# A hybrid decoder block on one core: a pinned first tile with zero products, first keys in double banks, and token sums whose low parts move to VectorE

## The chip, the core and the metric

The kernel runs on one core of a Trainium2 chip. The metric is the device time of one execution in microseconds; the time before is 1198.09, the median of three runs (1197.95 to 1198.48). PE is the matrix engine (TensorE), DVE is VectorE, ACT is ScalarE, POOL is GpSimd, SP is SyncE, which here only issues DMAs. A tile's name stands for its buffer; L95 is line 95 of the kernel before.

## What is computed

One layer: 16 meta tokens are put ahead of 512 tokens of width 1024, then

```
hn  = rmsnorm(h, norm_mix_pre)
rq, rk, rv, rg, sq, sk, sv, ga, gb = split(hn @ w_in)
y_ret = (silu(rg) * groupnorm(retention(rotary(rq), rotary(rk), rv))) @ w_ret_out
y_sb  = stick_breaking(sq, sk, sv) @ w_sb_out
h = h + rmsnorm((sigmoid(ga) * y_ret + sigmoid(gb) * y_sb) @ w_out, norm_mix_post)
h = h + rmsnorm(swiglu(rmsnorm(h, norm_ffn_pre)), norm_ffn_post)
```

with 4 retention heads (keys 256, values 512), 16 attention heads of 64 and an inner width of 2816. All is float32.

## The kernel before, in words

**Products in two parts.** Every operand is kept as a high part (the float32 number rounded to PE's fast form) and a low part (what is left). ACT makes the high part by a copy, DVE the low part by a subtraction (`split` at L103, `lo_of` at L100). One product is three on PE: high by high, high by low, low by high (L126 and L134, all issued at L95). Weights come in raw tiles of up to 1 MB (pool `wraw`, two buffers) and are split into units `wh` and `wl` (pool `wun`, five buffers of each). A raw buffer is free when all that reads it is done, a unit when PE has used it last; the next load or split waits for that.

**The order.** The program is written once and a scheduler with a timing model sets each engine's order, in which the engine then works strictly in sequence. Instructions marked with `tc.keep_in_program_order` stay in the order of the code. In the attention part all of PE is pinned so.

**The start (L648 to L715).** Gains of the first norm are brought into all partitions by transposes (`grow`, `gcol`, `gps`, L678 to L685). `innorm(i)` (L660) takes 128 tokens: ACT squares and sums a row (L666), DVE and POOL make the reciprocal root (L147, L148), DVE scales (hx, L671), PE transposes, and `split` writes the columns into hT and hL. Then come the values: `Values.load` loads 256 columns of w_in for four heads (L433), `part` multiplies one tile of tokens (L439), and `tail` the meta tokens. The first pair's queries and keys follow (`qk_work`, L487): queries in one PSUM bank of 512, keys in two halves of 264, evacuated by ACT into qa, qb, ka, kb and by DVE into the low parts, among them kl. Banks come from `bank_p` (two of 512) and from `bank_a` (two double ones).

**Token sums (L153 to L191).** The retention projections use a seven-product scheme on quarters, for which sums t1 to t4 of the normalised tokens are needed, split into th and tl. For each of four rows of feature tiles, `row_steps` issues ten POOL steps of 128x256 (L175) on hT and hL, then one ACT copy of 128x1024 (th, L184) and four POOL subtractions (tl, L185 and L186). These steps are handed out eight at a time between the attention's output products (L798 to L804), whose results DVE multiplies by a gate (gb, L801). The next user, `rv_proj(0)`, calls `tok_quarters` (L219): its four POOL sums in place, L233 to L236, prepare the weights' sums in the raw tiles. Its first two products use tokens as they are (`PRODUCTS`, L193), the third needs weights s2 and tokens t2. Then `ret_qk` (L898) multiplies and rotates queries and keys (`rotate`, L879: products with cosT and sinT into tiles rt, which read a PSUM bank that PE wants back), and the gate's `tok_quarters` makes its sums on POOL (L244, tile st).

**The tail (L1242 to L1257).** For each tile of 128 tokens the last products of two halves run; ACT squares and sums each half (L1249), DVE multiplies it by the last gains (fo, L1250), then the two sums make rs (L1252, L1253 on POOL), DVE finishes both halves (L1256) and SP writes them out.

Of the kernel before, what the change touches and what calls it, by code (L numbers as in the profile page):

```python
# [10 lines left out]
F32 = mybir.dt.float32  # L11
F32R = mybir.dt.float32r
# [4 lines left out]
P = 128  # L17
# [17 lines left out]
def hybrid_block(  # L35
# [32 lines left out]
    def bank_p():  # L68
        turns_p[0] += 1
        pool = third[0] if third and turns_p[0] % 3 == 0 else ps_p  # L70
        return pool.tile([P, 512], F32, tag="p", name="pp")

    def bank_a():
        return ps_a.tile([P, 2, 512], F32, tag="a", name="pa")
# [23 lines left out]
        return keep(nc.tensor.transpose(dst, src, idn))  # L98

    def lo_of(lo, src, hi):  # L100
        nc.vector.tensor_tensor(lo, src, hi.bitcast(F32), op=ALU.subtract)  # L101

    def split(hi, lo, src):  # L103
        ins = nc.scalar.activation(hi, src, AF.Copy)  # L104
# [48 lines left out]
    class Tokens:  # L153
# [15 lines left out]
        def row_steps(self, k, t, u):  # L169

            b11, b12, b21, b22 = [[v[:, k, :].bitcast(F32) for v in self.quarter(i, j)] for i in range(2) for j in range(2)]
            t1, t2, t3, t4 = [t[:, n, :] for n in range(4)]

            def op(d, p, q, o):
                tc.keep_in_program_order(nc.gpsimd.tensor_tensor(d, p, q, op=o))  # L175
# [8 lines left out]
            nc.scalar.activation(self.th[:, :, k, :], t, AF.Copy)  # L184
# [212 lines left out]
    with tc.tile_pool(name="s2", bufs=2, side=RS, reuse_waits="tile") as s2:  # L397
# [29 lines left out]
        class Values:  # L427
# [5 lines left out]
            def load(self):  # L433
# [2 lines left out]
                self.vt = vts[c] = s2.tile([P, NT, 4, P], F32R, tag="vt", name="vt")  # L436
                self.units = load_units(src, KD, 256, [(0, 4, 0, 256), (4, 4, 0, 256)])

            def part(self, js):  # L439
# [44 lines left out]
        qks = {}  # L484
        flat = lambda t: t.rearrange("p a b -> p (a b)")

        def qk_work(work, p, what="qk"):  # L487
            def q_load():
                return feat_units(w_in[:, O_SQ + P * p : O_SQ + P * (p + 1)])

            def q_steps(us):
                ps = bank_p()
# [12 lines left out]
            def k_steps(us):  # L505
                ka = s2.tile([P, 2, 264], F32R, tag="ka", name="ka", bufs=1)
                kb = s2.tile([P, 2, 264], F32R, tag="kb", name="kb")
                kl1 = kl1s[p % 2]
                for i in range(2):
                    cs = slice(264 * i, 264 * (i + 1))  # L510
                    pk = bank_p()[:, :264]
# [4 lines left out]
                    nc.scalar.activation(kb[0:64, i], pk[64:128], AF.Copy)  # L516
# [137 lines left out]
        def xload(i):  # L654
            if i == NT:
                nc.sync.dma_start(xts[i][:NM], meta)
            else:
                nc.sync.dma_start(xts[i], x[i * P : (i + 1) * P, :])

        def innorm(i):  # L660
            n = NM if i == NT else P
            c0 = 0 if i == NT else NM + i * P
            xt = xts[i]
            junk = bank_a().rearrange("p a b -> p (a b)")
            ss = cst.tile([P, 1], F32, name=f"ss{i}")
            nc.scalar.activation(junk[:n], xt[:n], AF.Square, accum_out=ss[:n])  # L666
            rstd_of(ss[:n], ss[:n], 1e-6, 1.0 / D, n)
            for j in range(2):
                hx = s2.tile([P, 512], F32, tag="qb", name="hx")
                cs = slice(512 * j, 512 * (j + 1))  # L670
                nc.vector.scalar_tensor_tensor(hx[:n], xt[:n, cs], ss[:n], gps[:n, j, :], op0=ALU.mult, op1=ALU.mult)  # L671
# [6 lines left out]
        nc.sync.dma_start(grow, g_mix_pre.rearrange("o (k p) -> (o k) p", p=P))  # L678
        xload(0)

        pg = bank_b()
        turned(pg[:, :KD], grow, ident[:KD, :KD])
        nc.scalar.activation(gcol, pg[:, :KD], AF.Copy)
        for k in range(KD):
            turned(gps[:, k // 4, (k % 4) * P : (k % 4 + 1) * P], gcol[:, k : k + 1].to_broadcast([P, P]), ident)  # L685
        vals = [Values(0), Values(1)]
        innorm(0)
        vals[0].load()
        xload(1)
        vals[1].load()  # L690
        innorm(1)
        for i in range(2, NT + 1):
            xload(i)
        work = Work()
        qk_work(work, 0)
        for j in range(NT):
            for v in vals:
                for _ in v.part((j,)):
# [73 lines left out]
    with tc.tile_pool(name="s3", bufs=1, side=RS, reuse_waits="tile") as s3:  # L772
# [20 lines left out]
        for f in range(0, KD, 2):  # L793
            if f:
                us = feat_units(w_sb_out[:, P * f : P * (f + 2)])
            gb = s3.tile([P, 2, T], F32, tag="gb", name="gb", bufs=2)
            nc.sync.dma_start(gb, gb_d[:, f : f + 2, :])
            for e in range(2):  # L798
                ps = bank_p()
                feat_mm(ps, us[e], lambda k: yh[:, k, :], lambda k: yl[:, k, :])  # L800
                nc.vector.tensor_tensor(gb[:, e, :], ps, gb[:, e, :], op=ALU.mult)  # L801
# [401 lines left out]
    with tc.tile_pool(name="s8", bufs=2, side=RS, reuse_waits="tile") as s8:  # L1203
# [38 lines left out]
        for i in range(NT):  # L1242
            sc, fo = [col("sc0"), col("sc1")], s8.tile([P, D], F32, tag="fo", name="fo")
            for c in range(2):
                for f in range(NF - REST, NF):
                    product(i, c, f)
                cs = slice(512 * c, 512 * (c + 1))
                sq = s8.tile([P, 512], F32, tag="sq", name="sq")
                nc.scalar.activation(sq, banks[i][c], AF.Square, scale=D**-0.5, accum_out=sc[c])  # L1249
                nc.vector.tensor_tensor(fo[:, cs], banks[i][c], gfin[:, cs], op=ALU.mult)  # L1250
            rs = col("rs")
            nc.vector.scalar_tensor_tensor(rs, sc[0], 1e-6, sc[1], op0=ALU.add, op1=ALU.add)  # L1252
            nc.gpsimd.tensor_tensor(rs, rs, nhalf, op=ALU.pow)  # L1253
            for c in range(2):
                cs = slice(512 * c, 512 * (c + 1))
                nc.vector.scalar_tensor_tensor(fo[:, cs], fo[:, cs], rs, h2[:, i, cs], op0=ALU.mult, op1=ALU.add)  # L1256
                nc.sync.dma_start(out[i * P : (i + 1) * P, cs], fo[:, cs])  # L1257
# [43 lines left out]
```

## Time and profile before

| | |
|---|---|
| median of three runs | 1198.09 us |
| profiled execution | 1197.83 us, its span 1196.0 us |
| PE busy | 1168.3 us (98%) |
| DVE busy | 851.2 us (71%) |
| ACT busy | 529.8 us (44%) |
| POOL busy | 348.7 us (29%) |
| mean granted clock of PE | 0.997 |

The page gives busy times and the slices of the span; the views by window give the same for single stretches. A timeline row has start, duration, engine, line, operation, tile out<-in, shape and count, and in brackets the engine's idle time ahead of it and what ended it. A row of the waits has the engine that waited and for whom, then us in total, times, and the longest.

### The profile page before, as it was taken

How to read it: one execution, taken by the hardware profiler on the slowest of the kernel's cores; microseconds unless marked ns; L12 is line 12 of the kernel's file. 1: busy time of each engine (PE TensorE's matmuls, PEld its weight loads, DVE VectorE, ACT ScalarE, POOL GpSimd, SP SyncE). 2: the span in 40 equal slices, each digit the busy share in tenths (PEclk: the TensorE clock that was granted, in tenths of full speed). 3: DMA queues.
4: the chain of work that ended last, by engine and by line, in shares of the span. 5: the costliest groups of instructions: out<-in, count | busy, mean ns of one | idle time of the engine just before them, and what ended most of it. 6: DMA issues, size and time to landing. Idle time of an engine off the chain costs nothing.

```text
span 1196.0 us, 18637 instructions
## 1 busy us (share of the span) xinstructions
PE 1168.3 (98%) x7521; PEld 1058.4 (88%) x7521; DVE 851.2 (71%) x1120; ACT 529.8 (44%) x899; POOL 348.7 (29%) x374
## 2 busy tenths in 40 slices
PE   7999999999999999999999999999999999999997
PEld 7988999988888988988898898788999999998886
DVE  5588788887447865687577657776799999983333
ACT  5476676666223434334243424344354444443321
POOL 2011122125864401340341120001366666620000
PEclk9999999999999999999999999999999999999999
DMA  6222222233532224122222414334132333253311
GB/s 196 84 85 89 63 64 73 75 99 110 190 116 71 81 71 141 36 81 100 78 73 79 141 54 141 132 135 139 44 106 81 114 98 130 84 185 106 103 39 71
DMA packets 98055, 118.24 MB, mean 99 GB/s; under 512 B 2584, under 2 KB 74272, under 8 KB 97968
## 3 DMA queue, kind: packets, MB, share of 16 engines
q1 hardware_dynamic: 97536, 115.98, 30.0%
q8 instruction: 59, 0.97, 0.3%
q10 hardware_dynamic: 432, 1.07, 0.3%
q14 instruction: 28, 0.23, 0.1%
HBM read 109.96 MB, written 7.08 MB: 98 GB/s over the span
## 4 chain that ended last, share of the span: by engine, by line
PE 76%; DVE 9%; POOL 6%; issue 4%; ACT 2%; DMA 2%; DVEq 0%; POOLq 0%; SPq 0%; ACTq 0%
PE pp L95 34%; PE pb L95 17%; PE pa L95 15%; PE pc L95 5%; DVE wl L101 3%; PE px L95 3%; PE pb L98 3%; DMA raw<-in_w_in_dram 2%; POOL ts L175 2%; POOL tl L175 2%; ACT wh L104 1%; DVE sm L574 1%; POOL raw L244 1%; POOL st L244 1%; DVE ub L266 1%
## 5 line engine op out<-in xcount | busy, mean ns | idle before, releaser
L101 DVE TENSOR_TENSOR wl<-raw,wh 128x1024 fp32r<-128x1024 f32 x196 | 265.9, 1363 | 79.5 <-ACT wh L104 76.1
L104 ACT ACTIVATE wh<-raw 128x1024 fp32r<-128x1024 f32 x196 | 196.9, 1013 | 209.0 <-PE pa L95 78.0
L95 PE MATMUL pp<-hT,wh 128*128 128x512 f32 (+1 forms) x320 | 116.5, 364 | 1.3 <-DVE qb L101 1.1
L95 PE MATMUL pp<-hL,wh 128*128 128x512 f32 (+1 forms) x320 | 112.3, 351 | 0.0
L95 PE MATMUL pp<-hT,wl 128*128 128x512 f32 (+1 forms) x320 | 112.1, 350 | 0.0
L101 DVE TENSOR_TENSOR wl<-st,wh 128x1024 fp32r<-128x1024 f32 x54 | 84.8, 1575 | 15.6 <-ACT wh L104 15.5
L244 POOL TENSOR_TENSOR st<-raw 128x512 f32<-128x512 f32 x28 | 43.6, 1579 | 159.8 <-DMA raw<-in_w_in_dram 159.8
L95 PE MATMUL pp<-qk,wh 128*128 128x512 f32 x256 | 83.2, 399 | 2.0 <-ACT qk L104 1.7
L95 PE MATMUL pp<-wh,hT 128*128 128x256 f32 (+1 forms) x240 | 75.0, 313 | 0.7 <-ACT hT L104 0.7
L95 PE MATMUL pp<-wh,hL 128*128 128x256 f32 (+1 forms) x240 | 74.4, 310 | 0.8 <-DVE ss L147 0.8
L95 PE MATMUL pp<-wl,hT 128*128 128x256 f32 (+1 forms) x240 | 73.9, 308 | 0.0
L104 ACT ACTIVATE wh<-st 128x1024 fp32r<-128x1024 f32 x54 | 56.0, 1055 | 35.5 <-POOL st L244 17.2
L95 PEld LDWEIGHTS pp<-hT,wl 128*128 128x128 f32 x320 | 60.2, 188 | 8.3
L584 POOL CAST mg<-sp 128x32 fp32r<-128x32 f32 x32 | 7.4, 230 | 204.5 <-DVE sp L575 155.1
L95 PEld LDWEIGHTS pp<-hT,wh 128*128 128x128 f32 x320 | 60.2, 188 | 7.5 <-issue 1.3
L95 PE MATMUL pa<-hT,wh 128*128 128x264 f32 (+1 forms) x192 | 62.4, 325 | 2.8 <-DVE rt L891 2.8
L95 PEld LDWEIGHTS pp<-hL,wh 128*128 128x128 f32 x320 | 60.4, 189 | 5.3
L574 DVE TENSOR_TENSOR_SCAN sm<-sm,mask 128x528 f32<-128x528 f32 (+1 forms) x64 | 54.9, 858 | 12.5 <-ACT sm L571 11.6
L148 POOL TENSOR_TENSOR rs<-rs,nhalf 128x1 f32<-128x1 f32 x20 | 12.7, 636 | 170.7 <-DVE rs L147 170.7
L95 PE MATMUL pa<-hL,wh 128*128 128x264 f32 (+1 forms) x192 | 62.2, 324 | 0.0
L95 PE MATMUL pa<-hT,wl 128*128 128x264 f32 (+1 forms) x192 | 62.1, 324 | 0.0
L95 PEld LDWEIGHTS pp<-qk,wh 128*128 128x128 f32 x256 | 47.6, 188 | 13.4 <-ACT qk L104 2.4
(326 smaller groups left out, 3726.8 us busy)
## 6 DMA issues: line engine op xcount, KB each, us to landing
raw<-in_w_in_dram SPq DMA_DIRECT2D x28, 1024.0 KB, 5.0
raw<-in_w_ffn_in_dram SPq DMA_DIRECT2D x22, 1024.0 KB, 5.1
raw<-in_w_in_dram SPq DMA_DIRECT2D x32, 512.0 KB, 4.2
raw<-in_w_ffn_out_dram SPq DMA_DIRECT2D x11, 1024.0 KB, 4.9
raw<-in_w_ret_out_dram SPq DMA_DIRECT2D x8, 1024.0 KB, 5.0
raw<-in_w_sb_out_dram SPq DMA_DIRECT2D x4, 1024.0 KB, 5.2
raw<-in_w_out_dram SPq DMA_DIRECT2D x4, 1024.0 KB, 5.0
ysb<-in_x_dram SPq DMA_DIRECT2D x4, 512.0 KB, 8.7
```

Of the source, the lines that this page charges most:

```text
L95: return keep(nc.tensor.matmul(*args, **kw))
L98: return keep(nc.tensor.transpose(dst, src, idn))
L101: nc.vector.tensor_tensor(lo, src, hi.bitcast(F32), op=ALU.subtract)
L104: ins = nc.scalar.activation(hi, src, AF.Copy)
L148: nc.gpsimd.tensor_tensor(dst, dst, nhalf[:n], op=ALU.pow)
L175: tc.keep_in_program_order(nc.gpsimd.tensor_tensor(d, p, q, op=o))
L244: nc.gpsimd.tensor_tensor(d[:, k : k + 2], p[:, k : k + 2], q[:, k : k + 2], op=op)
L266: nc.vector.tensor_tensor(ub[:, 1:4:2, :], p.rearrange("p (o n) -> p o n", o=1).to_broadcast([P, 2, n]), ub[:, 1:3, :], op=ALU.add)
L574: nc.vector.tensor_tensor_scan(rev, rev, mask[:, r0:][:, ::-1], 0.0, op0=ALU.mult, op1=ALU.max)
L584: nc.gpsimd.tensor_copy(g[:, two, 0:NM], m)
```

## The change

There are five parts.

1. **The first tile.** The first load of values goes out in two DMAs of 512 KB (`begin`) ahead of the second tile of tokens, and the gains' load moves from SP's queue to ACT's. The first tile's norm is shared: ACT squares half a row, DVE the other half, without the multiply-add step between. Its steps on ACT and DVE are pinned in a written order: square, first half of the weights, the tile, second half of the weights, then the second tile's square.
2. **Zero products.** Five products of zeros (128x512) on PE ahead of the gains' transposes, four behind them, into a bank that nothing reads.
3. **First keys.** Both halves of the first pair's keys go into `bank_a` (double banks); the queries stay in `bank_p`.
4. **Token sums.** The four POOL subtractions of a row become one DVE subtraction of 128x1024. A row has 11 steps handed out, not 14, and six go out at a time.
5. **The tail.** rs is made before the second half is multiplied by the gains.

```
 in row_steps:
             nc.scalar.activation(self.th[:, :, k, :], t, AF.Copy)
-            for n in range(4):
-                yield op(self.tl[:, n, k, :], t[:, n, :], self.th[:, n, k, :].bitcast(F32), ALU.subtract)
+            yield lo_of(self.tl[:, :, k, :], t, self.th[:, :, k, :])
...
-                for _ in range(8):
+                for _ in range(6):
                     next(token_sums, None)
 the start:
+            if i == 0:
+                so = cst.tile([P, 1], F32, name="so")
+                jv = s2.tile([P, 512], F32, tag="qb", name="jv")
+                tc.keep_in_program_order(nc.scalar.activation(junk[:, 0:512], xt[:, 0:512], AF.Square, scale=D**-0.5, accum_out=ss))
+                nc.vector.scalar_tensor_tensor(jv, xt[:, 512:D], 1.0 / D, xt[:, 512:D], op0=ALU.mult, op1=ALU.mult, accum_out=so)
+                nc.vector.scalar_tensor_tensor(ss, ss, 1e-6, so, op0=ALU.add, op1=ALU.add)
+                nc.gpsimd.tensor_tensor(ss, ss, nhalf, op=ALU.pow)
+                return
...
+        def first_tile(v):
+            pin = tc.keep_in_program_order
+            norm(0)
+            los = [v.take(0)]
...
+            los[0]()
+            for j in range(2):
+                ks = slice(4 * j, 4 * j + 4)
+                hi, lo = [v_[:, ks, NM : NM + P] for v_ in (hT, hL)]
+                pin(nc.scalar.activation(hi, pts[j], AF.Copy))
+                pin(lo_of(lo, pts[j], hi))
+            v.take(1)()
+            norm(1)
...
+        def idling(n):
+            for _ in range(n):
+                tc.keep_in_program_order(nc.tensor.matmul(idle, zeros[:, 0:P], zeros, start=True, stop=True))
+        idling(5)
...
+        idling(4)
+        first_tile(vals[0])
...
+        def first_bank():
+            kp.append(None)
+            return bank_a()[:, 0, :] if len(kp) > 1 else bank_p()
+        qk_work(work, 0, first_bank)
 the tail, in the loop over the two halves c:
                 nc.scalar.activation(sq, banks[i][c], AF.Square, scale=D**-0.5, accum_out=sc[c])
+                if c:
+                    rs = col("rs")
+                    nc.vector.scalar_tensor_tensor(rs, sc[0], 1e-6, sc[1], op0=ALU.add, op1=ALU.add)
+                    nc.gpsimd.tensor_tensor(rs, rs, nhalf, op=ALU.pow)
                 nc.vector.tensor_tensor(fo[:, cs], banks[i][c], gfin[:, cs], op=ALU.mult)
```

Here `v.take(i)` issues the high part of half i of the weights on ACT and returns the low part's step.

What the scheduler makes of it: apart from the stretches shown here, the first 30 us of PE and ACT, and a few weight splits on ACT and one load on SP near the token sums, the engines' orders stay as they were.

DVE at the start, before (ss with a number is the sum of one tile of tokens, the first of them tile 0; wl are weights, hL is a tile of tokens):

```order
L147 TENSOR_SCALAR ss_158<-ss_158 128x1
L671 SCALAR_TENSOR_TENSOR hx<-ysb,ss_158,pa 128x512 x2
L101 TENSOR_TENSOR wl<-raw,wh 128x1024 x2
L101 TENSOR_TENSOR hL<-pb,hT 128x4x128
L147 TENSOR_SCALAR ss_204<-ss_204 128x1
L101 TENSOR_TENSOR hL<-pb,hT 128x4x128
L671 SCALAR_TENSOR_TENSOR hx<-ysb,ss_204,pa 128x512 x2
```

and after:

```order
L742 MEMSET zeros 128x512
L779 MEMSET xm 128x8x16
L686 SCALAR_TENSOR_TENSOR jv,so<-ysb 128x512
L687 SCALAR_TENSOR_TENSOR ss_175<-ss_175,so 128x1
L719 SCALAR_TENSOR_TENSOR hx<-ysb,ss_175,pa 128x512 x2
L101 TENSOR_TENSOR wl<-raw,wh 128x1024
L101 TENSOR_TENSOR hL<-pb,hT 128x4x128 x2
L101 TENSOR_TENSOR wl<-raw,wh 128x1024
L147 TENSOR_SCALAR ss_209<-ss_209 128x1
L704 SCALAR_TENSOR_TENSOR hx<-ysb,ss_209,pa 128x512 x2
L101 TENSOR_TENSOR wl<-raw,wh 128x1024 x2
```

Only one half of the weights' low parts now stands ahead of the first tile's low parts.

POOL at the end of the token sums, before (ts and tu are the sums' rows, raw the weights of rv_proj(0)):

```order
L233 TENSOR_TENSOR raw<-raw 128x4x256
L175 TENSOR_TENSOR ts<-hT,ts 128x256
L234 TENSOR_TENSOR raw<-raw 128x4x256
L175 TENSOR_TENSOR ts<-ts,hL 128x256
L235 TENSOR_TENSOR raw<-raw 128x4x256
L175 TENSOR_TENSOR tl<-ts,th 128x256 x4
L236 TENSOR_TENSOR raw<-raw 128x4x256
```

and after, with new line numbers:

```order
L175 TENSOR_TENSOR ts<-hT,ts 128x256
L175 TENSOR_TENSOR ts<-ts,hL 128x256
L232 TENSOR_TENSOR raw<-raw 128x4x256
L233 TENSOR_TENSOR raw<-raw 128x4x256
L234 TENSOR_TENSOR raw<-raw 128x4x256
L235 TENSOR_TENSOR raw<-raw 128x4x256
```

The tl steps are gone from POOL, and the weights' four sums stand together behind the last row.

DVE among the attention's output products, after (before, the same rows stand without tl, with gb at L801):

```order
L101 TENSOR_TENSOR wl<-raw,wh 128x1024
L101 TENSOR_TENSOR tl<-ts,th 128x4x256
L876 TENSOR_TENSOR gb<-pp,gb 128x512
L101 TENSOR_TENSOR wl<-raw,wh 128x1024
L101 TENSOR_TENSOR tl<-ts,th 128x4x256
L876 TENSOR_TENSOR gb<-pp,gb 128x512
L101 TENSOR_TENSOR wl<-raw,wh 128x1024
```

Each tl stands ahead of a gb step. These are the third and the fourth row's, ahead of the fourth and the fifth product's gb.

More of the change, by code (lines that the diff above doesn't have):

```diff
@@ L437, in load, with begin, take @@
                 self.units = load_units(src, KD, 256, [(0, 4, 0, 256), (4, 4, 0, 256)])
+            def begin(self):
+                c = self.c
+                src = w_in[:, O_SV + 256 * c : O_SV + 256 * (c + 1)].rearrange("(k p) c -> p k c", p=P)
+                self.vt = vts[c] = s2.tile([P, NT, 4, P], F32R, tag="vt", name="vt")
+                self.raw = wraw.tile([P, KD, 256], F32, tag="raw", name="raw")
+                self.units = []
+                for i in range(2):
+                    nc.sync.dma_start(self.raw[:, 4 * i : 4 * (i + 1)], src[:, 4 * i : 4 * (i + 1)])
+            def take(self, i):
+                raw = self.raw[:, 4 * i : 4 * (i + 1)]
+                u = [wun.tile([P, 4, 256], F32R, tag=n, name=n) for n in ("wh", "wl")]
+                self.units.append(u)
+                tc.keep_in_program_order(nc.scalar.activation(u[0], raw, AF.Copy))
+                return lambda: tc.keep_in_program_order(lo_of(u[1], raw, u[0]))
             def part(self, js):
@@ L485, in hybrid_block, with qk_work @@
         flat = lambda t: t.rearrange("p a b -> p (a b)")
-        def qk_work(work, p, what="qk"):
+        def qk_work(work, p, bank=bank_p, what="qk"):
             def q_load():
@@ L491, in q_steps @@
             def q_steps(us):
-                ps = bank_p()
+                ps = bank()
                 yield from feat_steps(ps, us[0], xtok, ltok)
@@ L510, in k_steps @@
                     cs = slice(264 * i, 264 * (i + 1))
-                    pk = bank_p()[:, :264]
+                    pk = bank()[:, :264]
                     yield from feat_steps(pk, us[0], lambda k: hT[:, k, cs], lambda k: hL[:, k, cs])
@@ L658, in xload, with norm @@
                 nc.sync.dma_start(xts[i], x[i * P : (i + 1) * P, :])
+        def norm(i):
+            n = NM if i == NT else P
+            xt = xts[i]
+            junk = bank_a().rearrange("p a b -> p (a b)")
+            ss = rss[i] = cst.tile([P, 1], F32, name=f"ss{i}")
+            if i == 0:
[6 more added lines that the diff above has]
+                return
+            ins = nc.scalar.activation(junk[:n], xt[:n], AF.Square, accum_out=ss[:n])
+            if i == 1:
+                tc.keep_in_program_order(ins)
+            rstd_of(ss[:n], ss[:n], 1e-6, 1.0 / D, n)
+        rss = {}
         def innorm(i):
@@ L662, in innorm @@
             c0 = 0 if i == NT else NM + i * P
[L663 to L667, printed above, removed]
+            xt, ss = xts[i], rss[i]
             for j in range(2):
@@ L693, in hybrid_block @@
             xload(i)
+            norm(i)
         work = Work()
-        qk_work(work, 0)
+        kp = []
+        def first_bank():
+            kp.append(None)
+            return bank_a()[:, 0, :] if len(kp) > 1 else bank_p()
+        qk_work(work, 0, first_bank)
         for j in range(NT):
```

29 lines of the change are left out of this document (19 added, 10 removed).

## The prediction

> **What bounds the kernel now.** I read the page first, then PE's waits, then the timelines of the five places where PE waits and the change reaches. The page:
>
> ```profile
> span 1196.0 us, 18637 instructions
> ...
> PE 1168.3 (98%) x7521; PEld 1058.4 (88%) x7521; DVE 851.2 (71%) x1120; ACT 529.8 (44%) x899; POOL 348.7 (29%) x374
> ```
>
> PE is busy nearly always. A change that takes no product away can only win where PE waits or runs at half rate. PE's own waits, of which these matter here:
>
> ```profile
> PE pb L95 <- DVE ub L266: 3.8, 3, 1.8
> ...
> PE pa L95 <- DVE wl L101: 0.7, 1, 0.7
> PE pb L95 <- DVE wl L101: 0.6, 1, 0.6
> ```
>
> Columns: us in total, times, longest. The ub waits lie in the retention heads, where nothing changes. The change reaches the causes of the two wl waits, the start, one wait at the first keys, one before a rotation, and the tail.
>
> **The start.** The timeline of the first 23 us:
>
> ```profile
> 0.73 0.39 SPq L678 DMA_DIRECT2D grow<-in_norm_mix_pre_dram  x1
> 1.17 0.35 SPq L658 DMA_DIRECT2D ysb<-in_x_dram  x1
> 5.10 1.03 ACT L666 ACTIVATE pa<-ysb 128x1024 f32<-128x1024 f32 x1 [1.90 <-DMA ysb<-in_x_dram]
> 7.11 1.41 DVE L671 SCALAR_TENSOR_TENSOR hx<-ysb,ss,pa 128x512 f32<-128x512 f32 x2 [0.67 <-POOL ss L148]
> 8.08 2.00 ACT L104 ACTIVATE wh<-raw 128x1024 fp32r<-128x1024 f32 x2 [1.83 <-DMA raw<-in_w_in_dram]
> 9.17 2.36 DVE L101 TENSOR_TENSOR wl<-raw,wh 128x1024 fp32r<-128x1024 f32 x2 [0.65 <-ACT wh L104]
> 12.12 0.69 DVE L101 TENSOR_TENSOR hL<-pb,hT 128x512 fp32r<-128x512 f32 x1
> 16.83 0.41 PE L95 MATMUL pp<-wh,hL 128*128 128x256 f32 x1
> 17.05 0.41 PE L95 MATMUL pp<-wh,hT 128*128 128x256 f32 x1
> 18.75 0.28 PE L95 MATMUL pp<-wh,hL 128*128 128x256 f32 x1
> 18.87 0.28 PE L95 MATMUL pp<-wh,hT 128*128 128x256 f32 x1
> 22.15 0.36 PE L95 MATMUL pp<-wh,hL 128*128 128x256 f32 x1
> ...
> 24.00:28.00 4.00, 4.00 (x37) 4.00 (x35) 1.77 (x3) 0.98 (x2) 0.00 (x0) 1.00 0.08 23
> ```
>
> Two things are late. Products of 256 columns start 0.22 us apart up to 17.05 and 0.12 us apart from 18.75: until about 17 PE runs at half rate (the clock column doesn't show it here, the spacing does). And DVE does the low parts of the weights ahead of those of the first tile (12.12). From 22.15 on PE streams (37 products in 4 us, the last row, by stretches) until the keys.
>
> New order, DVE as the chain, durations from these rows. The gains' load leaves SP, so x is issued 0.44 earlier and lands at about 4.66. Half a square on ACT has no row here; bounds are half of 1.03 and, from the tail's row below, 0.60, plus 0.19 for reading the sum. The other half on DVE costs about one hx step (1.41/2 = 0.7). So the sums stand at 5.45, the power (0.55, a row of the tail below) ends at 6.3, hx x2 at 7.75, the first wl (2.36/2) at 8.95, hL x2 at 10.3, the second wl at 11.5. The second tile's square and power hold DVE until 12.5; hx x2 to 13.9, wl x2 to 16.3, vt (half an hL or so) and hL (0.69) to 17.5. PE finishes the first parts of both value halves at about 17.8 and goes on with the second tile, where it now stood at 22.15. Two products and four transposes (0.65) that were done by then still lie ahead: 22.15 - 17.8 - 0.65 = 3.7. DVE is busy throughout and two evacuations arrive just in time, so I take **3.4** (2.2 to 4.2).
>
> The nine zero products end by about 3.6 and 7.9 even at half rate (0.43 each, twice a 256-column product at 0.22); the transposes they could delay wait for hx until 7.1, so they cost at most 0.8, inside the above. [...]
>
> **The first keys.** Timeline:
>
> ```profile
> 53.31 0.28 PE L95 MATMUL pp<-hT,wl 128*128 128x264 f32 x1
> 54.67 0.36 PE L95 MATMUL pp<-hT,wh 128*128 128x264 f32 x1 [1.08 <-DVE qb L101]
> ...
> 61.02 0.42 DVE L101 TENSOR_TENSOR kl<-pp,ka 64x264 fp32r<-64x264 f32 x1 [0.39 <-ACT kb L516]
> ...
> 62.54 0.28 PE L95 MATMUL px<-ka,qa 128*128 128x264 f32 x1
> ```
>
> The second half of the keys waits for the bank that the queries still hold. In double banks it starts at once: 54.67 - 53.31 - 0.12 = 1.24. But the scores need kl, which ends at 61.44 behind ACT's copies, and ACT's queue need not run earlier for this; PE would be there at 61.3 (62.54 - 1.24), a hair too soon, and what ACT does next for the scores slips against PE. I take **0.8** (0.3 to 1.2).
>
> **The token sums.** Sixteen tl steps leave POOL, four of four times the size go to DVE. Timelines and the tile ts (ns min/median/max):
>
> ```profile
> 309.33 3.81 POOL L175 TENSOR_TENSOR tl<-ts,th 128x256 fp32r<-128x256 f32 x4 [1.17 <-ACT th L184]
> 314.66 1.78 DVE L101 TENSOR_TENSOR wl<-raw,wh 128x1024 fp32r<-128x1024 f32 x1 [0.17 <-ACT wh L104]
> 319.42 0.69 DVE L801 TENSOR_TENSOR gb<-pp,gb 128x512 f32<-128x512 f32 x1 [2.98 <-PE pp L95]
> ...
> 325.91 1.23 DVE L101 TENSOR_TENSOR wl<-raw,wh 128x1024 fp32r<-128x1024 f32 x1
> 346.84 2.93 POOL L236 TENSOR_TENSOR raw<-raw 128x1024 f32<-128x1024 f32 x1
> 349.80 3.21 SPq L112 DMA_DIRECT2D raw<-in_w_in_dram  x2
> ...
> L175 POOL TENSOR_TENSOR ts<-hT x8: 732/735/1727, 280.0 to 329.9; 128x256 f32<-128x256 f32 x8
> ```
>
> POOL works from 280.0 to 349.8 and the last step, L236, frees the buffer for the next weights: the load leaves at 349.80. Of that, tl is four times about 4 us with waits for th such as 1.17. Without them the 40 row steps (0.77 each, my estimate from 0.74 and the hop, 31 us, and 1 us, 1.73 against 0.74, for each of some nine DVE steps that collide) end near 320. The four raw sums then wait for the last split of their weights, at 327.1 (325.91 and 1.23), and end near 338 (four by 2.4 to 2.9): 12 us earlier. So the weights that PE awaits (0.7 and 0.6) are split in time: the two waits with their refilling are **1.6** (0.8 to 1.9).
>
> DVE pays 4 x 1.2 to 1.8 us. It has room, but its queue is in order: tl waits for ACT's th and so for POOL's row, with gb and the next wl behind it, and PE needs gb's bank two products later. The last tl stands ahead of the gb at 319.42; PE wants that bank one product later, at about 325.0. With th (1.06), tl and gb that allows the row until about 321.7; I have 320. Thin, yet nothing lost.
>
> [...]
>
> **The wait before the rotation.** One chain further:
>
> ```profile
> 379.31 1.23 DVE L101 TENSOR_TENSOR wl<-st,wh 128x1024 fp32r<-128x1024 f32 x1 [2.98 <-ACT wh L104]
> ...
> 364.57 3.53 POOL L244 TENSOR_TENSOR st<-raw 128x512 f32<-128x512 f32 x2 [14.79 <-DMA raw<-in_w_in_dram]
> ...
> 378.21 1.06 ACT L104 ACTIVATE wh<-st 128x1024 fp32r<-128x1024 f32 x1 [5.07 <-POOL st L244]
> ...
> 382.99 0.59 PE L95 MATMUL pa<-hT,wh 128*128 128x264 f32 x1 [2.81 <-DVE rt L891]
> ...
> 382.00:384.00 2.00, 1.01 (x4) 1.02 (x5) 1.97 (x4) 1.58 (x2) 0.00 (x0) 0.69 0.00 0
> 384.00:386.00 2.00, 2.00 (x11) 2.00 (x10) 2.00 (x4) 0.63 (x1) 0.00 (x0) 0.50 0.00 0
> 386.00:388.00 2.00, 2.00 (x17) 2.00 (x17) 0.55 (x1) 0.00 (x0) 0.00 (x0) 0.95 0.00 0
> ```
>
> DVE idles 2.98 us before wl<-st, which stands ahead of the rotation that frees PE's bank; wl waits for ACT, ACT for POOL's st, and POOL for gate weights (14.79 idle, on a DMA) whose buffer is freed behind the load of 349.80. With that load 10 us earlier they come about 8 us earlier (the slots that PE frees cap it), so wl could start near 371.3, and DVE reaches it at 379.31 - 2.98 - 1.6 = 374.7. Then nothing waits. PE regains 2.81, and half of the 3.4 us at clock 0.50 that follow (0.69, 0.50 and 0.95 over 2 us each), 1.7. With the refill that is **4.6** (0 to 4.7).
>
> **The tail.**
>
> ```profile
> 1189.92 0.19 ACT L1249 ACTIVATION_READ_ACCUMULATOR sq<-pc 128x1 f32 x1
> 1190.15 0.69 DVE L1250 TENSOR_TENSOR fo<-pc,gfin 128x512 f32<-128x512 f32 x1 [2.00 <-ACT sq L1249]
> ...
> 1190.99 0.55 POOL L1253 TENSOR_TENSOR rs<-rs,nhalf 128x1 f32<-128x1 f32 x1 [4.89 <-DVE rs L1252]
> 1191.57 1.41 DVE L1256 SCALAR_TENSOR_TENSOR fo<-fo,rs,h 128x512 f32<-128x512 f32 x2 [0.66 <-POOL rs L1253]
> ```
>
> rs now goes ahead of the second fo, whose 0.69 runs beside the power's 0.55. The pair at 1191.57 starts near 1191.1: **0.5** (0.4 to 0.6).
>
> **Sum.** 3.4 + 0.8 + 1.6 + 4.6 + 0.5 = 10.9. The profiled execution took 1197.83 (span 1196.0 and 1.8 around it), 0.26 under the median 1198.09, so the forecast is 1186.9 for such an execution and **1187.2** as a median. About 0.2% (2.4 us) is what a measurement of this kernel can tell from no change.
>
> **Rivals.** (1) The rotation's wait stays: another step of DVE's fixed order ahead of it is late, such as the split after a slot that PE frees. For: DVE's order there is unchanged. Against: over 3 us of slack in my chain. 4.6 go: 1191.8. [...] (3) Slower: tl stops DVE's queue. If every POOL row step ran at its collided 1.73, the 40 would end at 349, PE would wait 27 us for gb's bank, POOL's gain and all behind it would be gone, and 27 - 4.7 makes 1220. It decides from a mean of 1.04 us a step (wait begins) and turns the sign at about 1.3. Against it: the median step is 0.74, and mine with all collisions 1.0. [...] (4) The change does little: the PE waits merely move to the next wait for a load; 1196.5.
>
> **Chances.** Forecast with (2) inside its range 0.80; (1) 0.14; (3) 0.03; (4) 0.03. Range: the upper end must take in (1), 1192.2; the lower end, all terms at their best (13 with part of the waits for ub), 1184.8. Faster by over 0.2%: 0.94; within: 0.03; slower: 0.03.
>
> **What would show it.** Right: first tl and hL steps in the new order with the second tile's products from about 18 us at 0.12 spacing; no PE wait at 53; POOL's L236 twin ending near 338 less the shift; no PE wait on rt and no clock of 0.50 near 380; the last pair 0.5 closer to the last product. Wrong: DVE gb steps waiting behind tl with PE idle near 325; a PE wait on rt that stays; half-rate products after 12 us.

## The result, and the profile after

The changed kernel takes 1188.66 us (median of 5 runs, 1188.61 to 1190.56). The kernel before took 1198.23 beside it (5 runs, 1197.95 to 1200.78). The ratio is 0.9915, with a 95% interval of 0.9904 to 0.9926. The forecast was 1187.2, with a range of 1184.8 to 1192.2. The profiled execution took 1188.66; the page's first lines:

```profile
span 1186.8 us, 18647 instructions
...
PE 1166.4 (98%) x7530; PEld 1056.2 (89%) x7530; DVE 856.5 (72%) x1127; ACT 529.7 (45%) x899; POOL 336.5 (28%) x358
```

The span is 9.2 us shorter (1196.0 to 1186.8), where the sum of the prediction was 10.9. To see where, I set the same product of PE side by side in the two executions and noted by how much it comes earlier:

| Stretch | forecast | gain measured | PE is ahead by |
|---|---|---|---|
| start, to the first gates at 30 us | 3.4 | 3.80 | 3.80 |
| first keys, to the first turns at 76 us | 0.8 | -0.59 | 3.21 |
| token sums' rows, 325 us | 0 | -1.19 | 2.02 |
| the two waits for wl, 345 and 351 us | 1.6 | 1.79 | 3.81 |
| rotation, 383 to 386 us | 4.6 | 4.50 | 8.31 |
| everything up to the last product | 0 | 0.35 | 8.66 |
| tail | 0.5 | 0.54 | 9.20 |

Four of the five terms came out near their sizes. The keys lost time instead of winning it, and a wait came up in the token sums that the sum had at nothing. PE's waits after the change name both places (us in total, times, longest):

```profile
PE pb L98 <- DVE al L101: 2.5, 2, 1.8
PE pp L95 <- ACT wh L104: 1.2, 1, 1.2
```

The wait for rt and those of pa and pb for wl are gone from this list.

**The start.** Timeline of the changed kernel:

```profile
4.60 0.60 ACT L685 ACTIVATE pa<-ysb 128x512 f32<-128x512 f32 x1 [0.20 <-DMA ysb<-in_x_dram]
...
6.54 1.40 DVE L719 SCALAR_TENSOR_TENSOR hx<-ysb,ss,pa 128x512 f32<-128x512 f32 x2 [0.96 <-PE pa L98]
...
10.43 1.23 DVE L101 TENSOR_TENSOR wl<-raw,wh 128x1024 fp32r<-128x1024 f32 x1
...
13.72 2.35 DVE L101 TENSOR_TENSOR wl<-raw,wh 128x1024 fp32r<-128x1024 f32 x2
```

The square on x starts at 4.60 (worked out: 4.66). The first hx starts at 6.54 (worked out: 6.3); it waits 0.96 for the gains' transposes, which now stand behind the zero products. From there DVE follows the chain that I worked out: the second wl ends at 11.66 (11.5), the pair of the other half at 16.07 (16.3). The zero products raised PE's rate by 7.73: the gains' transposes stand 0.21 us apart up to 6.00 and the zero products 0.43 up to 7.50, but the transposes of hx 0.11 from 7.73 on; without the zero products (a run below) the half rate lasts until about 12.8.

**The first keys.** Before the change ACT's stretch looked so:

```profile
61.01 1.28 ACT L571 ACT_TABLE_LOAD   x1
...
62.98 0.39 ACT L571 ACTIVATE sm<-px 128x264 f32<-128x264 f32 x1 [0.69 <-PE px L95]
...
63.97 1.26 DVE L574 TENSOR_TENSOR_SCAN sm<-sm,mask 128x528 f32<-128x528 f32 x1 [2.05 <-ACT sm L571]
...
75.96 0.55 PE L98 MATMUL pb<-ident,sp 128*128 128x128 f32 x3 [0.46 <-DVE al L101]
```

and after it:

```profile
57.93 0.36 PE L95 MATMUL px<-ka,qa 128*128 128x264 f32 x1 [0.32 <-DVE kl L101]
...
58.48 1.28 ACT L587 ACT_TABLE_LOAD   x1 [1.60 <-PE px L95]
...
59.77 0.39 ACT L587 ACTIVATE sm<-px 128x264 f32<-128x264 f32 x1
...
60.76 1.26 DVE L590 TENSOR_TENSOR_SCAN sm<-sm,mask 128x528 f32<-128x528 f32 x1 [2.98 <-ACT sm L587]
...
72.75 0.55 PE L98 MATMUL pb<-ident,sp 128*128 128x128 f32 x3 [1.81 <-DVE al L101]
```

The load of the sigmoid's table (1.28) is what differs. Before, it ran at 61.01 right behind the last key copy and waited for nothing; the scores came at 62.54 and sm could begin at 62.98. After, it waits 1.60 for the scores themselves and runs between them and sm. ACT's order of instructions shows why (before, then after; in brackets the engines whose semaphores an instruction waits for):

```
46 L571 ACT_TABLE_LOAD
47 L571 ACTIVATE sm_127<-px 128x264 [waits PE_49]
```

```
47 L587 ACT_TABLE_LOAD [waits DVE_49,PE_49]
48 L587 ACTIVATE sm_127<-px 128x264 [waits Activation_49]
```

With the keys in the double banks the first sm has three waits, not one, and two of them stand on the load in front of it.

**The token sums.** The trace of before has no counterpart to this; timeline after:

```profile
302.78 1.06 ACT L104 ACTIVATE wh<-raw 128x1024 fp32r<-128x1024 f32 x1 [3.78 <-DMA raw<-in_w_sb_out_dram]
...
318.99 0.74 POOL L175 TENSOR_TENSOR ts<-ts,hL 128x256 f32<-128x256 f32 x1
319.76 1.06 ACT L184 ACTIVATE th<-ts 128x1024 fp32r<-128x1024 f32 x1 [7.46 <-POOL ts L175]
320.73 1.99 ACT L104 ACTIVATE wh<-raw 128x1024 fp32r<-128x1024 f32 x2
320.86 1.22 DVE L101 TENSOR_TENSOR tl<-ts,th 128x1024 fp32r<-128x1024 f32 x1 [6.38 <-ACT th L184]
322.00 0.69 DVE L876 TENSOR_TENSOR gb<-pp,gb 128x512 f32<-128x512 f32 x1
...
322.83 0.47 PE L95 MATMUL pp<-yh,wh 128*128 128x512 f32 x1 [1.19 <-ACT wh L104]
```

The profile names ACT's wh for PE's wait at 322.83. But the wh of this product was split at 302.78, by the buffer numbers in the order; the pair at 320.73 belongs to the weights after it. PE's first product also waits for DVE, and gb ended at 322.69: DVE had stood 6.38 us at tl, which waited for POOL's last row, with gb behind it. A run below (gb ahead of the last tl) bears this out: there the same product starts at 321.70, before the second split of that pair (323.44 there). The page counts 1.19 of idle time; from start to start, less the usual 0.23, PE loses 1.35.

**The rotation and the tail.** Here the forecast came true. The chain ahead of the rotation, then a stretch near it (the clock is the third figure from the end), show no wait of PE and no half clock:

```profile
334.90 2.81 DVE L101 TENSOR_TENSOR wl<-raw,wh 128x1024 fp32r<-128x1024 f32 x2
337.78 0.38 SPq L112 DMA_DIRECT2D raw<-in_w_in_dram  x1
...
371.72 1.23 DVE L101 TENSOR_TENSOR wl<-st,wh 128x1024 fp32r<-128x1024 f32 x1 [0.67 <-ACT wh L104]
...
374.68 0.69 DVE L966 TENSOR_TENSOR rt<-pa,cosT 128x512 f32<-128x512 f32 x1
```

```profile
376.00:378.00 2.00, 2.00 (x19) 2.00 (x18) 2.00 (x4) 0.89 (x2) 0.00 (x0) 1.00 0.02 4
```

The load leaves 12 us earlier than before (337.78, not 349.80), 2 to 4 of them by PE's lead. POOL's sums ended sooner still, at 335.50; the load then waited for the split of the same weights on DVE, to 337.71. So the margin was thin: DVE still idles 0.67 ahead of wl<-st, and the rt that frees the bank ends at 375.37, where PE wants it at 376.10.

In the tail the sum stands ahead of the second product with the gain:

```profile
1181.49 0.16 DVE L1327 SCALAR_TENSOR_TENSOR rs<-sc,sc 128x1 f32<-128x1 f32 x1 [2.03 <-ACT sq L1324]
1181.57 0.68 DVE L1329 TENSOR_TENSOR fo<-pc,gfin 128x512 f32<-128x512 f32 x1
1181.73 0.55 POOL L1328 TENSOR_TENSOR rs<-rs,nhalf 128x1 f32<-128x1 f32 x1 [4.89 <-DVE rs L1327]
1182.31 1.41 DVE L1332 SCALAR_TENSOR_TENSOR fo<-fo,rs,h 128x512 f32<-128x512 f32 x2
```

From the start of the last product (1188.94 before, 1180.28 after) to the last pair it is 2.63 before and 2.03 after.

### The profile page after: what moved, and what is told of

The parts are those of the page before. It is cut to its first block, busy times and chain, and to the rows that moved or that the text cites. A ratio compares the mean times of both kernels' runs of the same rounds, so it can differ in the third digit from the quotient of the medians.

```text
span 1186.8 us, 18647 instructions
## 1 busy us (share of the span) xinstructions
PE 1166.4 (98%) x7530; PEld 1056.2 (89%) x7530; DVE 856.5 (72%) x1127; ACT 529.7 (45%) x899; POOL 336.5 (28%) x358
## 3 DMA queue, kind: packets, MB, share of 16 engines
q10 hardware_dynamic: 448, 1.07, 0.3%
## 4 chain that ended last, share of the span: by engine, by line
PE 66%; DVE 3%; POOL 2%; issue 1%; ACT 1%; DMA 0%; DVEq 0%; POOLq 0%; ACTq 0%; SPq 0%
PE pp L95 24%; PE pb L95 18%; PE pa L95 18%; PE pc L95 5%; DVE wl L101 2%; PE pb L98 1%; POOL raw L243 1%; POOL st L243 1%; DMA raw<-in_w_in_dram 0%; ACT wh L104 0%; DVE ub L265 0%; DVE ub L259 0%; ACT qk L104 0%; DVE smt L101 0%; DVE tm L1005 0%
## 5 line engine op out<-in xcount | busy, mean ns | idle before, releaser
L95 PE MATMUL pp<-hT,wh 128*128 128x512 f32 (+1 forms) x304 | 112.0, 368 | 0.2 <-ACT ga L1125 0.2
L95 PE MATMUL pp<-hL,wh 128*128 128x512 f32 (+1 forms) x304 | 107.7, 354 | 0.0
L95 PE MATMUL pp<-hT,wl 128*128 128x512 f32 (+1 forms) x304 | 107.7, 354 | 0.0
L104 ACT ACTIVATE wh<-st 128x1024 fp32r<-128x1024 f32 x54 | 55.7, 1054 | 31.6 <-POOL st L243 19.3
L95 PE MATMUL pa<-hL,wh 128*128 128x264 f32 (+1 forms) x208 | 66.2, 318 | 0.0
L95 PE MATMUL pa<-hT,wh 128*128 128x264 f32 (+1 forms) x208 | 66.2, 318 | 0.0
L95 PE MATMUL pa<-hT,wl 128*128 128x264 f32 (+1 forms) x208 | 66.1, 318 | 0.0
L590 DVE TENSOR_TENSOR_SCAN sm<-sm,mask 128x528 f32<-128x528 f32 (+1 forms) x64 | 54.9, 858 | 13.6 <-ACT sm L587 12.8
L95 PEld LDWEIGHTS pp<-hT,wl 128*128 128x128 f32 x304 | 57.2, 188 | 8.3
L95 PEld LDWEIGHTS pp<-hT,wh 128*128 128x128 f32 x304 | 57.3, 188 | 6.2 <-ACT ga L1125 0.5
L95 PEld LDWEIGHTS pp<-hL,wh 128*128 128x128 f32 x304 | 57.4, 189 | 5.3
```

The costliest lines, as they stand in the source:

```text
L95: return keep(nc.tensor.matmul(*args, **kw))
L590: nc.vector.tensor_tensor_scan(rev, rev, mask[:, r0:][:, ::-1], 0.0, op0=ALU.mult, op1=ALU.max)
```

## The experiments

Three sets of four kernels ran, each set on one chip; the kernel before took 1198.87, 1198.13 and 1197.39 beside them, and 1198.23 beside the changed kernel. The ratios have intervals of about 1.5 us to either side. A difference of 1 to 1.5 us between two medians is therefore not shown by the times alone; where I claim one, I give what PE gains at that place, the same product in both traces. All edits are to the changed kernel; "the repaired kernel" is the one with both repairs below.

**One bank for the keys.** The undone part:

```diff
-        qk_work(work, 0, first_bank)
+        qk_work(work, 0)
```

> The changed kernel with its first keys back in the banks of the queries; all else as changed. Theory: the double banks cost 0.6 us net, since the sigmoid's table load (1.28 us), which ran behind the key copies without a wait before, now stands behind the first scores; with one bank PE waits about 1.2 us for the second half of the keys again, the table load is hidden again, the 1.8 us wait at the transposes near 73 us shrinks to about 0.4, and the time is 0.4 to 0.7 us below the changed kernel's 1188.66. Rival: what PE waits for near 73 us is set by loads or by DVE's queue whatever the banks, and the double banks did win their 1.2 us first; then the time is 0.3 to 1.2 us above the changed kernel's.

Measured: 1189.64 (1189.14 to 1189.89), 1.0 slower than the changed kernel (in the traces PE loses 0.99 between 25 and 73 us), so my theory had the sign wrong for this kernel. The rival's number came, but not for its reason. The trace has two waits at the keys:

```profile
51.41 0.36 PE L95 MATMUL pp<-hT,wh 128*128 128x264 f32 x1 [1.22 <-DVE qb L101]
55.74 0.47 PE L95 MATMUL pp<-hT,wh 128*128 128x512 f32 x1 [1.18 <-DVE kl L101]
```

The second was not there before the change. Every third call for a pp bank gets a bank of its own; the zero products take one call, so the first gate product (128x512) lost that bank and waits for the keys' one. The edit had undone the banks, not the turn. The next kernel sets it right.

**One bank, and the turn restored.**

```diff
-        qk_work(work, 0, first_bank)
+        qk_work(work, 0)
...
         idle = bank_p()
+        turns_p[0] -= 1
```

> The changed kernel with its first keys in the queries' banks as before, and the counter of bank turns set back by the one turn that the zero products took, so that the first gate product gets the third bank again, as it did before the change. Theory: the wait of 1.3 us at 55.7 that appeared with one bank is that lost turn and goes; the wait of 1.2 at the second half of the keys stays, the table load is hidden, the wait at the transposes is about 0.5; counted from 25 us on, PE is 0.4 to 0.7 us ahead of the changed kernel, and the time is 0.3 to 0.7 below 1188.66. Rival: the double banks are a gain by themselves, table load or not; then it is 0.3 to 1.2 above.

Measured: 1188.40 (1187.61 to 1188.60). In the trace the wait at 55.7 is gone, the one for qb is 1.20, the table load runs at 57.17 without a wait, and al is waited for 0.49. From 25 us to 73 us PE wins 0.46 us on the changed kernel. Together with the early table, next, this bears out the theory's mechanism; the median alone (0.26 lower) would not, since the ranges touch.

**The table early.** One sigmoid at the head of ACT's queue, so that the load at the scores falls away:

```diff
+        early = s2.tile([P, 1], F32, name="early", bufs=1)
+        tc.keep_in_program_order(nc.scalar.activation(early, nhalf, AF.Sigmoid))
         idling(5)
```

> The changed kernel with one sigmoid of 128x1 put at the start of ACT's queue, so that the sigmoid's table is loaded once, before x lands, and not at the first scores. Theory: the first score copies start about 1.3 us sooner after the scores, DVE's chain of scans moves by as much, the 1.8 us wait at the transposes near 73 us shrinks to about 0.5, and the time is 1.1 to 1.4 us below the changed kernel's 1188.66, near 1187.4. Rival: the chain there is held by the load of the next weights or by DVE's own work; the gain is then below 0.3 us.

Measured: 1187.17 (1186.73 to 1187.32), 1.49 below the changed kernel. In the traces PE gains 0.88 between 25 and 73 us, so the rival (below 0.3) falls. Timeline:

```profile
58.47 0.36 PE L95 MATMUL px<-ka,qa 128*128 128x264 f32 x1 [0.67 <-DVE kl L101]
...
59.04 0.39 ACT L587 ACTIVATE sm<-px 128x264 f32<-128x264 f32 x1 [1.62 <-PE px L95]
...
60.03 1.26 DVE L590 TENSOR_TENSOR_SCAN sm<-sm,mask 128x528 f32<-128x528 f32 x1 [1.70 <-ACT sm L587]
```

No table load stands at the scores, and the copies (wh at 54.75 and 60.14) and the sigmoid sm (59.04) run with none between them. Though the scores come 0.54 later here (58.47, not 57.93), the scan starts 0.73 earlier, and the wait at the turns is 0.50, not 1.81.

**The table early, with one bank.** Both edits above.

> The run before with the early sigmoid table as well. Theory: with one bank the table load was hidden, so taking it away gives under 0.2 us; and against the double banks with the early table (1187.17) this is 0.5 to 0.9 slower, what the double banks are worth when nothing stands behind them. Rival: the early table is worth a us here too, and the banks nothing: within 0.2 of 1187.17.

Measured: 1188.13 (1187.65 to 1188.32). Against one bank without the early table it gains 0.27: the load was hidden there. Against the double banks with it, it is 0.96 slower by the medians of two different sets, but the two traces differ by only 0.25 between 25 and 73 us. So the double banks seem to be worth something once nothing stands behind them; how much isn't settled by these runs.

**gb ahead of the last tl.** DVE's tl and gb keep the order of the code, with eight row steps handed out at a time:

```diff
-            yield lo_of(self.tl[:, :, k, :], t, self.th[:, :, k, :])
+            yield tc.keep_in_program_order(lo_of(self.tl[:, :, k, :], t, self.th[:, :, k, :]))
...
-                nc.vector.tensor_tensor(gb[:, e, :], ps, gb[:, e, :], op=ALU.mult)
+                tc.keep_in_program_order(nc.vector.tensor_tensor(gb[:, e, :], ps, gb[:, e, :], op=ALU.mult))
...
-                for _ in range(6):
+                for _ in range(8):
```

> The changed kernel with the tl and gb steps of DVE kept in the order in which they are written, and row steps handed out eight at a time, so that the last tl stands behind the gb that it held up, not ahead of it. Theory: the 1.35 us for which PE waits near 321 us is the bank that this gb frees, held because tl waits for POOL's last row; the wait goes and the time is 1.1 to 1.5 us below the changed kernel's 1188.66, near 1187.4. Rival: it is the weight split on ACT behind th, which the profile names, or POOL's later sums that set the end of this stage; then PE waits as long near 321 us or a few us on, and the time is within 0.4 us of the changed kernel's.

Measured: 1187.50 (1186.92 to 1190.07), 1.16 below the changed kernel, and PE's wait is gone: in the traces PE gains 1.36 at this product. Timeline:

```profile
321.70 0.73 POOL L175 TENSOR_TENSOR ts<-ts,hL 128x256 f32<-128x256 f32 x1
321.90 0.69 DVE L876 TENSOR_TENSOR gb<-pp,gb 128x512 f32<-128x512 f32 x1 [1.68 <-PE pp L95]
322.47 1.06 ACT L184 ACTIVATE th<-ts 128x1024 fp32r<-128x1024 f32 x1 [5.31 <-POOL ts L175]
323.56 1.23 DVE L101 TENSOR_TENSOR tl<-ts,th 128x1024 fp32r<-128x1024 f32 x1 [0.97 <-ACT th L184]
```

POOL's last row even ends 2.7 us later here (322.43, not 319.73), and PE doesn't wait. So the row's end as such cost nothing; the gb behind tl did.

**Both repairs together.**

> Both repairs together, the early sigmoid table and gb ahead of the last tl. Theory: the two holes are far apart (73 us and 321 us) and add up: 2.3 to 2.8 us below the changed kernel's 1188.66, near 1186.1. Rival: a later wait that is set by a load takes back what the first one gains; then it is no better than the better of the two alone.

Measured: 1185.94 (1185.47 to 1186.08), 2.72 below the changed kernel; the ratio to before is 0.9894, with an interval of 0.9880 to 0.9907. The two holes add up: 1.49 and 1.16 by the medians, and in the traces PE gains 0.83 between 25 and 73 us and 1.35 near 321. Only one version below is as fast.

**tl back on POOL.** The token sums' part of the change undone (four tl steps a row on POOL, eight steps handed out at a time):

```diff
-            yield lo_of(self.tl[:, :, k, :], t, self.th[:, :, k, :])
+            for n in range(4):
+                yield op(self.tl[:, n, k, :], t[:, n, :], self.th[:, n, k, :].bitcast(F32), ALU.subtract)
...
-                for _ in range(6):
+                for _ in range(8):
```

> The changed kernel with the four tl steps of a row back on POOL, eight handed out at a time; all else as changed. Theory: the two waits for wl near 345 and 351 (1.8 together) and the wait with the half clock before the rotation (4.5) come back, the wait at 321 (1.35) goes; the time is 4.5 to 5.3 us above the changed kernel's 1188.66, near 1193.6. Rival: what ended the wait before the rotation was the earlier start of everything, not the earlier load; then the time is less than 2 us above.

Measured: 1193.58 (1191.71 to 1194.12), 4.92 above. The waits of before come back at their old places, and the half clock with them; the load leaves at 347.09. The wait and the stretches:

```profile
379.76 0.39 PE L95 MATMUL pa<-hT,wh 128*128 128x264 f32 x1 [2.29 <-DVE rt L967]
```

```profile
380.00:382.00 2.00, 2.00 (x14) 2.00 (x14) 2.00 (x4) 1.23 (x2) 0.00 (x0) 0.71 0.00 0
382.00:384.00 2.00, 2.00 (x11) 2.00 (x11) 1.32 (x2) 0.00 (x0) 0.00 (x0) 0.50 0.00 0
```

So the earlier load, and not the earlier start, ended the wait before the rotation.

**Where POOL's time went.** The eight yl steps replaced by fills with zeros:

```diff
-            split(yh[:, k, :], yl[:, k, :], ysb[:, k, :])
+            tc.keep_in_program_order(nc.scalar.activation(yh[:, k, :], ysb[:, k, :], AF.Copy))
+            nc.vector.memset(yl[:, k, :].bitcast(F32), 0.0)
```

> The changed kernel with the eight yl steps of DVE (the low parts of the heads' output) replaced by eight fills with zeros that read nothing: the low parts are left out of the products behind them. Theory: POOL's second row ran at 1.07 to 1.60 us a step because, freed of tl, it met the eight yl steps on DVE; without them its steps take 0.74, the last row ends 3 to 5 us before 319.7, the wait of 1.35 at 321 goes, and the time is 1.1 to 1.5 us below 1188.66. Rival: wl and tl alone make POOL slow; the last row ends within 1 us of 319.7 and the time stays within 0.4.

Measured: 1187.52 (1187.45 to 1187.90), 1.14 below; in the traces PE gains 1.35 near 321. One step of POOL's second row in the changed kernel, then the same one with the fills, and the end of the rows there:

```profile
285.91 1.20 POOL L175 TENSOR_TENSOR tu<-hL 128x256 f32<-128x256 f32 x1
```

```profile
285.31 0.73 POOL L175 TENSOR_TENSOR tu<-hL 128x256 f32<-128x256 f32 x1
...
315.94 0.73 POOL L175 TENSOR_TENSOR ts<-ts,hL 128x256 f32<-128x256 f32 x1
```

The rows end 3.06 earlier (316.67, not 319.73), and the wait at 321 is gone. A step takes 0.99 on average (40 steps from 277.05), where the changed kernel needs 1.07 (from 276.86); ten of them still take 1.6 to 1.8 beside wl and tl, in both kernels.

**Without zero products.**

```diff
-        idling(5)
+        idling(0)
...
-        idling(4)
+        idling(0)
```

> The changed kernel without its nine zero products; order and pins stay. Theory: PE then does its first transposes and products at half rate until about 13 us (0.22 us for a product of 256 columns, not 0.12); part of that hides behind the waits for wl and hL, and 0.8 to 2.0 us of the start's 3.8 are lost. Rival: DVE's chain sets the pace until 17 us at either rate, and under 0.4 us is lost.

Measured: 1191.86 (1190.55 to 1194.25), 3.2 slower; the profiled execution is one of its slowest (1194.24). But the start isn't where it goes. PE runs at half rate until about 12.8, products of 256 columns 0.21 us apart and then 0.12:

```profile
12.20 0.41 PE L95 MATMUL pp<-wh,hL 128*128 128x256 f32 x1
12.41 0.41 PE L95 MATMUL pp<-wh,hT 128*128 128x256 f32 x1
...
12.83 0.28 PE L95 MATMUL pp<-wh,hL 128*128 128x256 f32 x1
12.96 0.28 PE L95 MATMUL pp<-wh,hT 128*128 128x256 f32 x1
```

and yet the product that stands at 25.18 in the changed kernel stands at 25.24. The loss comes later. A load of weights that ACT splits ahead of the key copies arrives late: it is issued at the same time (49.37, and 49.42 in the changed kernel) but takes 6.70 to land, not 4.71. The keys are late with it, PE waits 2.21 for kl, and a clock of 0.50 follows (timeline, then a stretch).

```profile
56.15 1.06 ACT L104 ACTIVATE wh<-raw 128x1024 fp32r<-128x1024 f32 x1 [1.75 <-DMA raw<-in_w_in_dram]
...
59.87 0.36 PE L95 MATMUL px<-ka,qa 128*128 128x264 f32 x1 [2.21 <-DVE kl L101]
```

```profile
62.00:64.00 2.00, 2.00 (x6) 1.61 (x5) 1.26 (x1) 2.00 (x6) 0.00 (x0) 0.50 0.02 6
```

By 73 us PE has lost 1.9 to the changed kernel; this execution loses another 3.7 later, 2.2 of them near 520 us with a half clock (0.50 from 522 to 524); these runs don't show why. Was the late load an accident of the one program? The repaired kernel without zero products:

> The kernel with both repairs, without the nine zero products. Theory: the zero products did nothing for the start (without them PE stood at 25 us where it stands with them, though at half rate before 13 us, since DVE's chain sets the pace), and what the kernel without them lost came from one load of weights that landed 1.9 us late near 56 us; that is an accident of that program, and the time here is within 0.5 us of the repaired kernel's 1185.94. Rival: without them a load near 56 us is late every time, by what the start does to the transfers; then 2 to 4 us above 1185.94.

Measured: 1188.72 (1186.76 to 1190.46), 2.8 above the repaired kernel. The theory falls. The split of the same load comes 5.05 us after the one ahead of it (57.56 and 52.51), and 4.42 in the kernel above (56.15 and 51.73), against 2.6 to 3.1 in the changed kernel and in every other version of it here. So without the zero products that load is late in both profiled executions. Both are among the slowest of their runs (this one is the slowest, 1190.46), so whether it is late every time isn't shown. How nine products at 2 to 8 us could decide when a load at 50 us lands stays open; the time without them is longer in both programs.

**Fewer zero products.** Three ahead of the gains' transpose, not five, in the repaired kernel.

> The kernel with both repairs, with three zero products ahead of the gains' transpose in place of five. Theory: the gains' transposes come 0.5 us sooner, the first hx no longer waits for them (0.39 of its 0.96 us wait goes), and DVE's chain, which sets the pace to 17 us, is 0.3 us earlier: 0.2 to 0.4 below 1185.94. Rival: what sets the pace is the landing of the weights; within 0.15 of 1185.94.

Measured: 1185.84 (1185.11 to 1187.42), the same as the repaired kernel. hx no longer waits for the transposes (0.67 behind POOL's power is left), but in the profiled execution x itself landed at 5.56 (4.60 in the changed kernel), so what this is worth can't be told from it.

**The tail undone.** The sum and the power back behind both products with the gain.

> The changed kernel with the sum and the power of the last norm back behind the second product with the gain, as before the change. Theory: the time from the last product to the end is 0.4 to 0.6 us longer, and the time 0.3 to 0.7 above 1188.66. Rival: the power on POOL hides behind the same step as before; within 0.2.

Measured: 1189.92 (1188.66 to 1191.75), 1.26 above. From the start of the last product to the end of the span it is 7.21 (1182.79 to 1190.0), against 6.52 (1180.28 to 1186.8): 0.69. What makes the rest of the 1.26 isn't settled. The profiled execution is the slowest of the five (1191.75); in it PE falls back at 25 us, at 58 us and, after a wait for ub, to the half clock at 626 us (0.50 from 627 to 629).

## Why the prediction was right, and where not

**The start** (3.4, measured 3.80) came in step with the chain that I gave, DVE's new order up to 17 us; its rows stand within 0.3 us of those worked out. No run undoes that order alone, so its share is argued from the rows. The chances take in a rival (2) on this stage, for which no run shows a term; what the runs showed is that PE's products of 256 columns stand 0.12 apart from 9.97 on, and that in the kernel without zero products PE runs at half rate until 12.8 and yet stands at 25.24 where it stood at 25.18, since DVE's chain hides it.

**The first keys** (0.8, measured -0.59) failed at the step "what ACT does next for the scores slips against PE". I saw a slip and took 0.4 for it. Up to the scores that was right: beyond the lead from the start, the second half of the keys came 1.23 sooner and the scores 0.81. But behind the scores stood the table load, 1.28 that the trace of before showed at 61.01 with nothing waiting for it. I had named no work that hides it, and the change took its cover away. Shown by the early table (PE's wait at the turns falls from 1.81 to 0.50) and by one bank with the turn restored (0.49).

**The token sums.** The 1.6 for the two waits was right (1.79), and the kernel with tl back on POOL confirms it with the rotation: 4.92 together, where 1.79 and 4.50 less 1.19 make 5.1. The step that failed is "that allows the row until about 321.7; I have 320". Both numbers were in the time of before. PE was 3.2 us ahead by then, so the deadline stood at 318.5; POOL's rows, which start with the heads' end, shifted along (276.86, not 280.0), so that my 320 meant 316.9. They ended at 319.73: I counted nine DVE steps that collide at about 1 us each (ten POOL steps do take 1.6 to 1.8), and left out the eight yl steps, which met POOL's second row only now that tl no longer held that row up. The third rival's estimate fits: it put the start of the wait at 1.04 a step, and at 1.07 over 40 steps the wait is 1.35. What that rival described, tl stopping DVE's queue, took place, at a size far from turning the sign.

**The rotation** (4.6, measured 4.50) came whole, and tl back on POOL brings the wait back. But the step "over 3 us of slack in my chain" failed: 0.73 were left on PE's side. My chain had POOL's last sum free the buffer; the load left 2.28 later than that, behind DVE's split of the same weights, and DVE still had to wait 0.67 for the wh of wl<-st. That the full term came is in part luck. Rival 1 did not come: no other step of DVE's order there was late enough to hold PE. **The tail** (0.5) measures 0.54 between the two profiles, and 0.69 by the part undone.

The forecast gain was thus too high by 1.7 of span: 1.4 at the keys, 1.2 at the token sums, less 0.9 at the start, the two waits and elsewhere.

## What to carry to other kernels

When a change moves work forward, look in the trace of before for everything that runs in the gap that it closes and that waits for nothing, a table load above all (1.28 us here): its cover is the gap. When a step goes to another engine, count the steps that now run beside the engine it left (here eight yl steps, beside which POOL's took 1.07 to 1.20 us and not 0.74), and put deadline and supply in the same shifted time. A late step costs by what stands behind it in its queue, not by its own lateness: putting gb ahead of tl was worth as much (1.36) as making POOL faster by leaving out yl (1.35). And a slack is safe only when every step that can free the buffer is in it.

## What the runs showed that I had not expected

- A wait can be carried by the table load ahead of the step that needs it: 1.60 us of waiting, then 1.28 of load. No further pause followed (58.48 and 1.28 make 59.76, sm began at 59.77). The changed kernel's trace has five table loads of 1.28 each; with the early sigmoid none runs between 48 and 64 us, where the changed kernel has the one at 58.48.
- Both sides of a collision slowed down: where yl and POOL's second row ran beside each other, yl took 1225 ns and not 678 in the median, POOL's step 1.07 to 1.20 us and not 0.74, and against DVE steps of 128x1024 (wl and tl) POOL's took 1.60 to 1.78. The yl steps before the change, then after:

```profile
L101 DVE TENSOR_TENSOR yl<-ysb,yh x8: 675/678/1228, 286.4 to 291.4; 128x512 fp32r<-128x512 f32 x8
```

```profile
L101 DVE TENSOR_TENSOR yl<-ysb,yh x8: 898/1225/1234, 283.3 to 291.0; 128x512 fp32r<-128x512 f32 x8
```

- The length of PE's pause alone did not decide about the half clock. Counted from the start of one product to the next, less the usual 0.12, pauses of 1.94 (tail undone, 622 us) and 1.97 (no zero products, 517 us) were followed by a clock of 0.50; pauses of 1.97 (changed kernel, 71 us) and 2.22 (repaired, no zero products, 517 us) were not (stretches of the first and of the last):

```profile
627.00:629.00 2.00, 2.00 (x12) 2.00 (x11) 1.91 (x5) 1.60 (x3) 0.55 (x1) 0.50 0.77 195
```

```profile
521.00:523.00 2.00, 2.00 (x17) 1.91 (x16) 1.97 (x5) 0.52 (x1) 0.20 (x1) 1.00 0.29 13
```

  What does decide it, no run here shows.
